# Row-by-row loads and stores on two DMA queues, in place of one queue in a written-out order, in a cross-entropy gradient kernel

## The chip, the cores and the metric

The kernel runs on one core of a Trainium2 chip. The metric is device time in microseconds (us), the median of the runs of one kernel. Beside the times there is one profiled execution, with a trace of every instruction and every DMA packet. Engines are named as in the profile: PE (matmul), DVE (vector), ACT (scalar), POOL (GpSimd), SP (the sync engine, which here does nothing but issue DMAs). A letter q behind an engine (SPq, ACTq) is its sequencer, the part that issues DMAs and waits on semaphores.

## The reference

The input is `logits`, 8 x 1024 rows of 8192 float32, and one integer label for each row. The output has the shape of `logits`: the softmax of each row, less one at the label's column.

```python
logits_max = np.max(logits, axis=-1, keepdims=True)
exp_logits = np.exp(logits - logits_max)
softmax = exp_logits / np.sum(exp_logits, axis=-1, keepdims=True)
one_hot[batch_idx, seq_idx, labels] = 1.0
return (softmax - one_hot).astype(np.float32)
```

268.4 MB are read and 268.4 MB are written, and nothing of the large input is needed twice.

## The kernel before, in words

The 8192 rows are cut into T = 64 tiles of 128 rows, one row on each of the 128 partitions. A tile is 128 x 8192 float32, that is 4 MB, 32 KB on each partition. Two tiles, 2b and 2b + 1, hold alternate rows of the same 256 (`"(b p j) v -> b p j v"` with j = 2), so that the two rows that one partition gets from such a pair lie side by side in memory, 64 KB in one piece.

All of the work is done in place in one buffer `X` with SLOTS = 6 slots of one tile each; tile t uses slot t % 6. For each tile there are five steps, in the function `compute`:

- `row_max`: DVE takes the negated maximum of each row into `m` (TENSOR_REDUCE).
- ACT computes exp(x + m) in place, and the row's sum `s` with it (ACTIVATE X<-X,m).
- DVE takes the reciprocal `r` of the sum.
- ACT multiplies the whole row by `r` in place (ACTIVATE X<-X,r). This is called the scaling below.
- DVE compares the column numbers with the row's label and subtracts the outcome from the row, in place (SCALAR_TENSOR_TENSOR X<-iota,lab,X). This is called the subtraction below.

The column numbers are 16-bit integers that stay in PSUM (`iota`); they are made once at the start in the last slot of X, which is therefore free for loads only when DVE has copied them out. On DVE the order is: reciprocal of tile t, maximum of tile t + 1, subtraction of tile t. The scaling of tile t on ACT so lies beside the maximum of tile t + 1 on DVE, and the exponential of tile t + 1 beside the subtraction of tile t. The last tile is scaled and subtracted in two halves.

No scheduler arranges anything here: the whole kernel is one critical section with semaphores set by hand. A helper, `run`, issues every instruction, with its waits ahead of it and a semaphore increment behind it. This is why nearly every instruction has the same line in the profile, L75, and why groups are told apart by their engine and tiles.

All large transfers are issued by SP on one queue, in the order that the string ORDER writes out: L is a load, S a store, the number is the tile, and W means two adjacent tiles in one transfer of 8 MB (64 KB runs in HBM):

```python
ORDER = """
L0 L1 L2W L4W S0 S1 L6 L7 S2 S3 L8 L9 S4W S6 L10W S7 S8
L12W S9 S10 L14W S11 S12 ... L52W S49 S50
L54 L55 S51 L56 S52W L57 L58 S54W L59 L60W S56 S57 L62 L63 S58W S60W S62 S63
"""
```

In the middle of the program this is one 8 MB load and two 4 MB stores in turn. SP waits at each entry for what it needs: a load for the stores that free its slots, a store for the subtraction of its tile. An entry that waits holds all entries behind it. There are 39 loads (14 of one tile, 25 of two) and 59 stores (54 and 5). The small load of the labels is issued by ACT at the start, on ACT's queue.

Of the kernel before, what the change touches and what calls it, by code (L numbers as in the profile page):

```python
# [6 lines left out]

P = 128  # L8
SLOTS = 6  # L9

ORDER = """
L0 L1 L2W L4W S0 S1 L6 L7 S2 S3 L8 L9 S4W S6 L10W S7 S8
L12W S9 S10 L14W S11 S12 L16W S13 S14 L18W S15 S16 L20W S17 S18 L22W S19 S20
L24W S21 S22 L26W S23 S24 L28W S25 S26 L30W S27 S28 L32W S29 S30 L34W S31 S32
L36W S33 S34 L38W S35 S36 L40W S37 S38 L42W S39 S40 L44W S41 S42 L46W S43 S44
L48W S45 S46 L50W S47 S48 L52W S49 S50
L54 L55 S51 L56 S52W L57 L58 S54W L59 L60W S56 S57 L62 L63 S58W S60W S62 S63
"""  # L20


@with_exitstack
def kernel(
    ctx: ExitStack,
    tc: tile.TileContext,
    logits: bass.AP,
    labels: bass.AP,
    out: bass.AP,
):  # L30
    nc = tc.nc
    fp32 = mybir.dt.float32
    i32 = mybir.dt.int32
    i16 = mybir.dt.int16
    Act = mybir.ActivationFunctionType
    Alu = mybir.AluOpType

    x_nv = logits.flatten_outer_dims()
    o_nv = out.flatten_outer_dims()
    N, V = x_nv.shape  # L40
    T = N // P
    G = 2
    B = T // G
    lab_bp = labels.rearrange("a b -> (a b)").rearrange("(b q) -> b q", q=G * P)
    x_b = x_nv.rearrange("(b p j) v -> b p j v", p=P, j=G)
    o_b = o_nv.rearrange("(b p j) v -> b p j v", p=P, j=G)

    const = ctx.enter_context(tc.tile_pool(name="const", bufs=1))
    psum = ctx.enter_context(tc.tile_pool(name="psum", bufs=1, space=bass.MemoryType.PSUM))


    X = const.tile([P, SLOTS, V], fp32)
    lab_raw = const.tile([B, G * P], labels.dtype)
    lab_f = const.tile([B, G, P], fp32)  # L54
    ident = const.tile([B, B], fp32)  # L55
    lab = const.tile([P, G, B], fp32)  # L56

    m, s, r = (const.tile([P, T], fp32, name=n) for n in ("m", "s", "r"))  # L58

    iota = psum.tile([P, V], i16)  # L60
    lab_ps = iota[:].bitcast(fp32)[:, :T].rearrange("p (j b) -> p j b", j=G)

    with tc.tile_critical():  # L63
        sem = tc.alloc_semaphore
        got = [sem(f"got{i}") for i in range(SLOTS)]
        put = [sem(f"put{i}") for i in range(SLOTS)]
        lab_got, dve, act, pe, pool = (sem(n) for n in ("lab_got", "dve", "act", "pe", "pool"))
        count = dict.fromkeys((x.name for x in (*got, *put, lab_got, dve, act, pe, pool)), 0)

        def run(engine, waits, counter, method, **operands):  # L70

            waits = list(dict.fromkeys(waits))
            for w in waits[:-1]:
                engine.wait_ge(*w)  # L74
            instruction = getattr(engine, method)(**operands)  # L75
            for w in waits[-1:]:
                instruction._wait_ge(*w)
            step = 16 if method == "dma_start" else 1
            instruction.then_inc(counter, step)
            count[counter.name] += step  # L80
            return counter, count[counter.name]


        w_raw = run(nc.scalar, [], lab_got, "dma_start", out=lab_raw[:], in_=lab_bp)
        w = run(nc.gpsimd, [], pool, "memset", ap=ident[:], constant=0.0)
        w_ident = run(
            nc.gpsimd, [w], pool, "affine_select",
            out=ident[:], in_=ident[:], compare_op=Alu.not_equal, fill=1.0,
            base=0, pattern=[[-1, B]], channel_multiplier=1,
        )  # L90

        made = X[:, SLOTS - 1, :].bitcast(i16)[:, :V]
        w_made = run(
            nc.gpsimd, [], pool, "iota", out=made, pattern=[[1, V]], base=0, channel_multiplier=0
        )
        step = mybir.dt.size(labels.dtype) // 4
        lab32 = lab_raw[:].bitcast(i32).rearrange("b (p j s) -> b j p s", j=G, s=step)
        w_lab = run(nc.vector, [w_raw], dve, "tensor_copy", out=lab_f[:], in_=lab32[:, :, :, 0])
        for j in range(G):
            w = run(  # L100
                nc.tensor, [w_ident, w_lab], pe, "transpose",
                out=lab_ps[:, j, :], in_=lab_f[:, j, :], identity=ident[:],
            )
        w = run(nc.vector, [w], dve, "tensor_copy", out=lab[:], in_=lab_ps)
        w_iota = run(
            nc.vector, [w, w_made], dve, "tensor_scalar",
            out=iota[:].bitcast(i32), in0=made.bitcast(i32), scalar1=0, scalar2=None, op0=Alu.bitwise_or,
        )


        loaded, stored, w_max, finished = {}, {-1: w_iota}, [], []

        def hbm(rows, t, n):
            b, j = divmod(t, G)
            return rows[b, :, j : j + n, :]

        def sbuf(t, n):
            return X[:, t % SLOTS : t % SLOTS + n, :]

        def load(t, n):  # L120
            free = [stored[u - SLOTS] for u in range(t, t + n) if u - SLOTS in stored]
            w = run(nc.sync, free, got[t % SLOTS], "dma_start", out=sbuf(t, n), in_=hbm(x_b, t, n))
            loaded.update(dict.fromkeys(range(t, t + n), w))

        def store(t, n):
            compute(t + n)
            w = run(
                nc.sync, [finished[t + n - 1]], put[t % SLOTS], "dma_start",
                out=hbm(o_b, t, n), in_=sbuf(t, n),
            )  # L130
            stored.update(dict.fromkeys(range(t, t + n), w))

        def row_max(t):
            w_max.append(run(
                nc.vector, [loaded[t]], dve, "tensor_reduce",
                out=m[:, t : t + 1], in_=X[:, t % SLOTS, :], axis=mybir.AxisListType.X, op=Alu.max, negate=True,
            ))

        def compute(end):

            for t in range(len(finished), end):
                x = X[:, t % SLOTS, :]
                if t == 0:
                    row_max(0)
                w = run(
                    nc.scalar, [w_max[t]], act, "activation",
                    out=x, in_=x, func=Act.Exp, bias=m[:, t : t + 1], scale=1.0, accum_out=s[:, t : t + 1],
                )
                w = run(nc.vector, [w], dve, "reciprocal", out=r[:, t : t + 1], in_=s[:, t : t + 1])
                if t + 1 < T:  # L150
                    row_max(t + 1)

                n = 1 if t + 1 < T else 2
                cols = [slice(i * V // n, (i + 1) * V // n) for i in range(n)]
                scaled = [
                    run(
                        nc.scalar, [w], act, "activation",
                        out=x[:, c], in_=x[:, c], func=Act.Copy, bias=0.0, scale=r[:, t : t + 1],
                    )
                    for c in cols  # L160
                ]
                for c, w in zip(cols, scaled):
                    w = run(
                        nc.vector, [w], dve, "scalar_tensor_tensor",
                        out=x[:, c], in0=iota[:, c], scalar=lab[:, t % G, t // G : t // G + 1], in1=x[:, c],
                        op0=Alu.is_equal, op1=Alu.subtract, reverse1=True,
                    )
                finished.append(w)

        for word in ORDER.split():  # L170
            n = 2 if word.endswith("W") else 1
            (load if word[0] == "L" else store)(int(word[1:].rstrip("W")), n)
        for w in dict.fromkeys(stored[t] for t in range(T - SLOTS, T)):
            nc.sync.wait_ge(*w)


# [28 lines left out]
```

## Time and profile before

| What | Value |
|---|---|
| Median of 3 runs | 1253.62 us (1253.48 to 1255.25) |
| The profiled execution's own time | 1253.48 us |
| Its span in the profile | 1251.7 us, 582 instructions |
| DVE busy | 1119.1 us, 196 instructions |
| ACT busy | 919.0 us, 194 instructions |
| POOL and PE busy | 7.4 us and 0.4 us |
| Moved between HBM and SBUF | 268.50 MB read, 268.44 MB written, 429 GB/s over the span |
| Granted clock | 1.0 |

The span is the time in which the profile shows instructions; the execution's own time is 1.78 us longer. Shares of busy time are averages over the span. The chain of work that ended last, which the profile follows back from the last instruction, tells which of the resources set the end. A DMA's packets are its pieces as the DMA engines carry them: here one packet for each partition of a transfer, of 32 KB or 64 KB, and a packet of 4 bytes for each of the 16 DMA engines that increments the semaphore.

### The profile page before, as it was taken

What the parts mean: (1) busy time and instruction counts of PE and PEld (TensorE: products, weight loads), DVE (VectorE), ACT (ScalarE), POOL (GpSimd) and SP (SyncE); (2) the same over time, 40 slices, a digit from 0 to 9 for tenths busy, and PEclk for the clock granted to TensorE, in tenths of its full rate; (3) what the DMA queues carried; (4) which work ended last, traced back from release to release, by engine and by line L of the source; (5) the groups of instructions that cost most, each with busy time, mean ns of one, the idle gap of its engine ahead of it and who ended that gap; (6) DMA issues with size and microseconds to landing.
All of it is one profiled execution on the core that took longest, in us unless ns stands there. A gap on an engine that the chain in (4) does not pass through costs nothing.

```text
span 1251.7 us, 582 instructions
## 1 busy us (share of the span) xinstructions
PE 0.4 (0%) x2; PEld 0.3 (0%) x2; DVE 1119.1 (89%) x196; ACT 919.0 (73%) x194; POOL 7.4 (1%) x7
## 2 busy tenths in 40 slices
PE   0000000000000000000000000000000000000000
PEld 0000000000000000000000000000000000000000
DVE  5999999888998889988899888898888989997993
ACT  3888887667777777777777777877768778887782
POOL 2000000000000000000000000000000000000000
DMA  9999999999999999999999999999999999999998
GB/s 404 419 436 431 438 422 435 434 427 431 430 448 434 418 429 436 441 421 430 430 435 439 434 431 426 432 450 429 425 429 436 437 427 432 419 424 436 435 436 354
DMA packets 14165, 536.98 MB, mean 429 GB/s; under 512 B 1584, under 2 KB 1584, under 8 KB 1616
## 3 DMA queue, kind: packets, MB, share of 16 engines
q1 hardware_dynamic: 14112, 536.88, 99.6%
q10 hardware_dynamic: 48, 0.07, 0.0%
q14 instruction: 5, 0.04, 0.0%
HBM read 268.50 MB, written 268.44 MB: 429 GB/s over the span
## 4 chain that ended last, share of the span: by engine, by line
DMA 58%; DVE 39%; ACT 1%; issue 0%; PE 0%; ACTq 0%; DVEq 0%; SPq 0%
DMA out_dram<-X 30%; DMA X<-in_logits_dram 28%; DVE X L75 19%; DVE m L75 19%; ACT X L75 1%; DVE iota L75 0%; DMA lab_raw<-in_labels_dram 0%; DVE lab_f L75 0%; DVE r L75 0%; PE iota L75 0%; DVE lab L75 0%; ACTq L200 0%; DVEq L74 0%; SPq L63 0%
## 5 line engine op out<-in xcount | busy, mean ns | idle before, releaser
L75 DVE TENSOR_REDUCE m<-X 128x1 f32<-128x8192 f32 x64 | 555.2, 8674 | 100.0 <-DMA X<-in_logits_dram 100.0
L75 ACT ACTIVATE X<-X,m 128x8192 f32<-128x8192 f32 x64 | 455.8, 7122 | 214.3 <-DVE m L75 214.3
L75 DVE SCALAR_TENSOR_TENSOR X<-iota,lab,X 128x8192 f32<-128x8192 int16 (+1 forms) x65 | 559.6, 8610 | 3.8 <-ACT X L75 3.8
L75 ACT ACTIVATE X<-X,r 128x8192 f32<-128x8192 f32 (+1 forms) x65 | 456.0, 7016 | 95.6 <-DVE r L75 95.6
L75 DVE RECIPROCAL r<-s 128x1 f32<-128x1 f32 x64 | 9.8, 153 | 7.3 <-ACT X L75 7.3
L75 ACT ACTIVATION_READ_ACCUMULATOR X<-X,m 128x1 f32 x64 | 11.9, 187 | 0.0
L75 DVE CAST lab_f<-lab_raw 32x256 f32<-32x256 int32 x1 | 3.7, 3661 | 4.7 <-DMA lab_raw<-in_labels_dram 4.7
L75 POOL IOTA X<- 128x8192 int16 x1 | 6.9, 6943 | 0.0
L75 DVE TENSOR_SCALAR iota<-X 128x4096 int32<-128x4096 int32 x1 | 4.4, 4428 | 0.1
L75 ACT ACT_TABLE_LOAD x1 | 1.3, 1283 | 1.3 <-SPq L63 1.3
L75 DVE COPY lab<-iota 128x64 f32<-128x64 f32 x1 | 0.2, 225 | 0.5 <-PE iota L75 0.5
L75 PE MATMUL iota<-ident,lab_f 32*128 32x32 f32 x2 | 0.4, 300 | 8.4 <-DVE lab_f L75 8.4
L75 PEld LDWEIGHTS iota<-ident,lab_f 32*128 32x128 f32 x2 | 0.3, 195 | 8.4 <-DVE lab_f L75 8.4
L75 POOL TENSOR_SCALAR_AFFINE_SELECT ident<-ident 32x32 f32<-32x32 f32 x1 | 0.2, 203 | 0.1
L75 POOL MEMSET ident<- 32x32 f32 x1 | 0.1, 114 | 0.5 <-SPq L63 0.5
L189 POOL MEMSET const-bfloat16-1.0<- 128x1 bf16 x1 | 0.1, 106 | 0.0
L189 POOL MEMSET const-uint8-127<- 128x1 uint8 x1 | 0.1, 106 | 0.0
L189 POOL MEMSET const-float32-0.0<- 128x1 f32 x1 | 0.1, 103 | 0.2 <-issue 0.2
L189 POOL MEMSET const-float32-1.0<- 128x1 f32 x1 | 0.1, 103 | 0.0
## 6 DMA issues: line engine op xcount, KB each, us to landing
out_dram<-X SPq DMA_DIRECT2D x54, 4096.0 KB, 24.9
X<-in_logits_dram SPq DMA_DIRECT2D x14, 4096.0 KB, 19.6
X<-in_logits_dram SPq DMA_DIRECT2D x25, 29.0
out_dram<-X SPq DMA_DIRECT2D x5, 26.6
lab_raw<-in_labels_dram ACTq DMA_DIRECT2D x1, 64.0 KB, 3.8
```

The lines of the kernel that those rows point to most:

```text
L75: instruction = getattr(engine, method)(**operands)
L189: nc = _bacc.Bacc("TRN2", target_bir_lowering=False, num_devices=1)
```

## The change

ORDER and everything that reads it go away. SP issues the 64 loads alone, one tile each, in the order of the tiles; a load waits for nothing but the store that frees its slot. The 64 stores, one tile each, are issued by ACT on its own queue. In ACT's stream the store of tile t - 1 stands between the exponential of tile t and the scaling of tile t, and waits there for the subtraction of tile t - 1. The final wait for the last six stores moves from SP to ACT. The order and the kind of the instructions on DVE, PE and POOL are the same as before, as are those on ACT apart from the stores. The layout of rows and the six slots stay, too. The helper's line is L64 in the new kernel.

```diff
-ORDER = """
-L0 L1 L2W L4W S0 S1 L6 L7 S2 S3 L8 L9 S4W S6 L10W S7 S8
...
-"""
         def store(t, n):
-            compute(t + n)
             w = run(
-                nc.sync, [finished[t + n - 1]], put[t % SLOTS], "dma_start",
+                nc.scalar, [finished[t + n - 1]], put[t % SLOTS], "dma_start",
                 out=hbm(o_b, t, n), in_=sbuf(t, n),
             )
...
-        def compute(end):
...
+        load(0, 1)
+        row_max(0)
+        for t in range(T):
+            x = X[:, t % SLOTS, :]
+            w = run(
+                nc.scalar, [w_max[t]], act, "activation",
+                out=x, in_=x, func=Act.Exp, bias=m[:, t : t + 1], scale=1.0, accum_out=s[:, t : t + 1],
+            )
+            w = run(nc.vector, [w], dve, "reciprocal", out=r[:, t : t + 1], in_=s[:, t : t + 1])
+            if t + 1 < T:
+                load(t + 1, 1)
+                row_max(t + 1)
+            if t > 0:
+                store(t - 1, 1)
...
-        for word in ORDER.split():
-            n = 2 if word.endswith("W") else 1
-            (load if word[0] == "L" else store)(int(word[1:].rstrip("W")), n)
+            finished.append(w)
+        store(T - 1, 1)
         for w in dict.fromkeys(stored[t] for t in range(T - SLOTS, T)):
-            nc.sync.wait_ge(*w)
+            nc.scalar.wait_ge(*w)
```

More of the change, by code (lines that the diff above doesn't have):

```diff
@@ L9 @@
 SLOTS = 6
-ORDER = """
-L0 L1 L2W L4W S0 S1 L6 L7 S2 S3 L8 L9 S4W S6 L10W S7 S8
[L15 to L19, printed above, removed]
-"""
 @with_exitstack
@@ L137, in row_max @@
             ))
-        def compute(end):
[L141 to L144, printed above, removed]
+        load(0, 1)
[12 more added lines that the diff above has]
+                store(t - 1, 1)
+            n = 1 if t + 1 < T else 2
+            cols = [slice(i * V // n, (i + 1) * V // n) for i in range(n)]
+            scaled = [
+                run(
+                    nc.scalar, [w], act, "activation",
+                    out=x[:, c], in_=x[:, c], func=Act.Copy, bias=0.0, scale=r[:, t : t + 1],
+                )
+                for c in cols
+            ]
+            for c, w in zip(cols, scaled):
@@ L145, in compute @@
                 w = run(
-                    nc.scalar, [w_max[t]], act, "activation",
-                    out=x, in_=x, func=Act.Exp, bias=m[:, t : t + 1], scale=1.0, accum_out=s[:, t : t + 1],
-                )
[L149 to L167, printed above, removed]
@@ L168, in compute @@
-                finished.append(w)
-        for word in ORDER.split():
-            n = 2 if word.endswith("W") else 1
-            (load if word[0] == "L" else store)(int(word[1:].rstrip("W")), n)
+                    nc.vector, [w], dve, "scalar_tensor_tensor",
+                    out=x[:, c], in0=iota[:, c], scalar=lab[:, t % G, t // G : t // G + 1], in1=x[:, c],
+                    op0=Alu.is_equal, op1=Alu.subtract, reverse1=True,
+                )
+            finished.append(w)
+        store(T - 1, 1)
```

## The prediction

> **What bounds the kernel now.** I read the page's busy line, its DMA lines and queues first, then the chain of waits, then windows by stage, and the timeline where the stores begin.
>
> ```profile
> PE 0.4 (0%) x2; PEld 0.3 (0%) x2; DVE 1119.1 (89%) x196; ACT 919.0 (73%) x194; POOL 7.4 (1%) x7
> DMA packets 14165, 536.98 MB, mean 429 GB/s; under 512 B 1584, under 2 KB 1584, under 8 KB 1616
> q1 hardware_dynamic: 14112, 536.88, 99.6%
> ```
>
> The 16 DMA engines carry SP's queue (q1) for 99.6% of the span; DVE comes next with 89%. The chain agrees, and the waits show who is behind:
>
> ```profile
> DMA 58%; DVE 39%; ACT 1%; issue 0%; PE 0%; ACTq 0%; DVEq 0%; SPq 0%
> ...
> DVE m L75 <- DMA X<-in_logits_dram: 100.0, 25, 4.9
> SPq L75 <- DVE r L75: 733.5, 55, 33.0
> SPq L75 <- DMA out_dram<-X: 444.1, 32, 33.1
> ```
>
> DVE waits for loads 25 times, 100.0 us in all: it is 100 us quicker than the transfers. SP's long waits cost nothing while the queue still holds a transfer. By stage, in the windows (the last two columns are the DMA share and GB/s):
>
> ```profile
> 168.00:638.00 470.00, 0.00 (x0) 0.00 (x0) 417.18 (x75) 344.32 (x73) 0.00 (x0) 1.00 1.00 432
> 638.00:986.00 348.00, 0.00 (x0) 0.00 (x0) 312.17 (x55) 257.79 (x54) 0.00 (x0) 1.00 1.00 434
> 986.00:1100.00 114.00, 0.00 (x0) 0.00 (x0) 108.97 (x21) 91.96 (x19) 0.00 (x0) 1.00 1.00 426
> 1200.00:1252.00 52.00, 0.00 (x0) 0.00 (x0) 31.77 (x7) 25.74 (x7) 0.00 (x0) 1.00 0.88 379
> ```
>
> Only start and end lie below 426 GB/s. So the time is bytes, by the rate of the engines, plus small losses. The trace's packet records give these. The median 32 KB packet takes 1.213 us, the 64 KB one 2.418, the 4-byte one 0.009; a load's packet and a store's are equal. For one of 16 engines: 8704/16 x 1.213 + 3840/16 x 2.418 + 98 x 0.009 = 659.9 + 580.3 + 0.9 = 1241.1 us. The records sum to 1247.1, so 6.0 us are excess over the medians: 0.3 in the first packets, 5.7 later. The first large packet starts at 2.2, the last ends at 1249.9: 1247.7 us, of which 0.6 idle. After it 1.8 us are left to the span's end, and the execution's time lies another 1.8 above the span. The median of the runs is 0.14 above this execution.
>
> **The change, part by part.** *Smaller transfers.* All 128 are of one tile, where 98 were: 1024 packets of 1.213 and 128 of 0.009 on each engine, 1242.1 + 1.2 = 1243.3 us, 2.2 more than 1241.1. Nothing covers this, since these engines are the bound.
>
> *The stores on ACT.* An issue takes 0.33 us on SP (row below) and 0.41 on ACT (the labels' load). In the timeline at the first store:
>
> ```profile
> 38.20 8.74 DVE L75 SCALAR_TENSOR_TENSOR X<-iota,lab,X 128x8192 f32<-128x8192 int16 x1
> 38.31 7.12 ACT L75 ACTIVATE X<-X,m 128x8192 f32<-128x8192 f32 x1 [1.46 <-DVE m L75]
> ...
> 46.85 0.15 DVE L75 RECIPROCAL r<-s 128x1 f32<-128x1 f32 x1
> 46.92 8.67 DVE L75 TENSOR_REDUCE m<-X 128x1 f32<-128x8192 f32 x1
> ...
> 47.04 7.12 ACT L75 ACTIVATE X<-X,r 128x8192 f32<-128x8192 f32 x1 [1.51 <-DVE r L75]
> ...
> 1129.76 0.34 SPq L75 DMA_DIRECT2D out_dram<-X  x1
> ```
>
> The new wait on ACT is for the subtraction of tile t - 1; behind it are queued the scaling of t and the exponential of t + 1. But the scaling waits for the reciprocal of t, which DVE runs just after that very subtraction (46.85 behind 38.20 + 8.74), so the wait ends no later than one that ACT had. Only the issue is new: the scaling starts 0.4 us late, at 47.4, and ends at 54.5, while DVE is in its maximum until 55.6. The 1.46 us that ACT waits for that maximum are the cover. Without it, it would be 63 x 0.41 = 26 us of ACT, still within DVE's 100 us of waiting. I take 0. On SP, 64 loads stay; none is behind a store any more.
>
> *The freed order.* A load waits for its slot alone. In the steady stage let a load land at A. Maximum 8.7, then the subtraction of the tile before 8.7 (it stands behind that maximum), then the wait for the next load at A + 19.4 (two 4 MB transfers of 8 x 1.213 = 9.7 each), then 17.4 again: the store is issued at A + 36.8. A slot comes round every 6 x 19.4 = 116.4 us, so 79.6 remain for its store and next load; sharing the engines by halves each takes 19.4, 38.8 together. Some 40 us are spare, less a few for issue and landing: a second transfer waits in each queue most of the time, and the engines never run dry. What is late next is the DMA again.
>
> *The end.* When stores begin, at 47, 4.6 loads are done; 1.4 remain, and at half rate the last lands 27 us later. That lead of 27 us from a load's issue to its landing then keeps itself, since a load is issued as often as a store lands. So tile 63 lands 27 us after store 57, with 4.6 stores still to do: 45 us. DVE needs only 8.7 + 7.2 for maximum and exponential, the older subtraction until 17.4, then halves of 3.7, 4.4 and 4.4: the last store is issued at 30, and three stores lie ahead of it until 35. No idle: 0.
>
> *Load and store packets in turn.* Today the queue changes direction 59 times (counted in ORDER). Afterwards both queues are busy for all but 4.6 loads at the start and 4.6 stores at the end: 118.8 transfers, 950 packets on each engine. The trace never has two large streams at once, so I bound the price by its changes. All excess behind the first packets put on the 59 changes is 5.7/59 = 0.096 us for each and engine; in the even stretch from 638 to 986 us it is 0.49 us for 18 changes, 0.027. The changes afterwards number 950, if the engines alternate by packet, or 119, if by whole transfer. The four products are 3.2, 11.4, 25.6 and 91 us. Below nothing: a load writes SBUF while a store reads it, so two streams could overlap; the end of that is DVE's own time. Its last subtraction ends at 1235.5; less 100.0 of waits 1135.5, plus 14.7 to the landing of a store (shortest of the DMA view) and 1.5: a span of 1152, 96 us below 1247.6, the sum below before this term. The equal packets of both directions speak for a cap inside the engine and so against such a gain. Between the four products, with no row nearer to one than to another, I take their geometric middle, 17 us.
>
> The Trainium skill, page "DMA: Bandwidth & Descriptors", section "Queues, rings and completion order", says that an engine goes round its queues packet by packet, a packet there being typically 9 to 17 descriptors. A transfer here has 8 pieces and one semaphore write on each engine, so by that rule it would be the coarse count, 3 to 11 us, and a time of about 1253 to 1261; no view of before shows two large queues at once.
>
> *Sum.* 2.2 (start) + 0.3 (first packets) + 1243.3 + 17 + 1.8 = 1264.6 us of span; + 1.8 + 0.14 gives 1266.5.
>
> **The rivals.** *Alternation is free.* The 5.7 us of excess and 0.6 of idle belong to the old queue's restarts and vanish: 2.2 + 0.3 + 1243.3 + 1.8 = 1247.6, a time of 1249.5, 4.1 below before. For it: between 638 and 986 us nine cycles of one 8 MB load and two stores take 348.36/9 = 38.71 us against 38.78 of packet work, though each has two changes. Against: in the stretch before, twelve take 39.13. It decides below 4.1 us for 950 packets, 4.3 ns each: then the change is a gain. Chance 0.20 (0.14 a gain over 0.2%, 0.06 within).
>
> *The directions overlap.* Down to 1152 + 1.9 = 1154 if DVE is the bound. Chance 0.06.
>
> *Stores get more than half.* Then a load's lead grows, and little is left to store when tile 63 lands. With only stores 62 and 63 left, the engines idle from store 62's end (17.4 + 9.7) to 30 and before 17.4: 20 us, 1249.5 + 20 = 1269.5. For it: nothing seen; against: equal packets. It decides below 3.1 stores left. Chance 0.06.
>
> *Every change at the dearer price, by packet:* 1249.5 + 91 = 1341. Against: the even stretch has 0.027. Chance 0.08.
>
> The change does what it says: the order of instructions shows 64 loads on SP and 64 stores on ACT.
>
> **How the numbers follow.** The forecast, alternation at a price of 3 to 60 us, has 0.60 and by itself reaches from 1253 to 1310; 0.04 of it lies within 0.2% (2.5 us, about what a measurement of this kernel can tell from no change). Faster: 0.14 + 0.06 = 0.20. Same: 0.06 + 0.04 = 0.10. Slower: 0.56 + 0.06 + 0.08 = 0.70. The range goes from 1247, under the free rival, to 1305; outside lie 0.06 below, and above it the 0.08 and some 0.04 of the forecast.
>
> **What would show it.** The forecast: two queues of about 268 MB each, a mean near 424 GB/s, DVE's wait for loads up from 100 to about 115 us, and 32 KB packets whose excess is spread evenly from 50 to 1220 us. Wrong about ACT: the scaling shows up late in DVE's waits (DVE X on ACT far over 3.8 us). Wrong about the end: an idle DMA in the last two slices beyond today's 354 GB/s. Wrong altogether: a rate of 430 GB/s or more in the middle, or DVE without waits for loads.

## The result, and the profile after

The changed kernel is faster, by half a per cent: 1248.1 us median (1247.97 to 1248.16, 4 runs) against 1254.2 for the kernel before beside it, a ratio of 0.9951 with a 95% interval of 0.9933 to 0.9968. A later set of runs gave 1248.12 against 1254.31, ratio 0.9950 (0.9937 to 0.9962). The forecast was 1266.5 and slower. The rival "alternation is free" had said 1249.5, with a chance of 0.14 for a gain of this size. The time lies inside the range of 1247 to 1305, on the other side of the kernel before.

The page's busy line, the slices, and the packets by queue (number, MB, share of the 16 engines' span):

```profile
span 1246.4 us, 592 instructions
PE 0.4 (0%) x2; PEld 0.3 (0%) x2; DVE 1121.3 (90%) x196; ACT 919.0 (74%) x194; POOL 7.4 (1%) x7
...
GB/s 406 418 430 433 435 434 430 433 435 433 431 434 434 433 431 434 434 432 431 434 435 432 431 434 434 431 433 434 435 431 433 433 434 432 432 433 435 431 432 385
DMA packets 18484, 536.98 MB, mean 431 GB/s; under 512 B 2064, under 2 KB 2064, under 8 KB 2096
q1 hardware_dynamic: 9216, 268.44, 50.0%
q10 hardware_dynamic: 9264, 268.51, 49.9%
```

The bytes are the same, and each queue carries half. The DMA engines are as full as before, 99.9% in sum, but no slice from the third to the last but one is below 430 GB/s. The same stages as before, in the windows:

```profile
168.00:638.00 470.00, 0.00 (x0) 0.00 (x0) 435.90 (x78) 361.18 (x76) 0.00 (x0) 1.00 1.00 433
638.00:986.00 348.00, 0.00 (x0) 0.00 (x0) 312.64 (x55) 257.20 (x55) 0.00 (x0) 1.00 1.00 433
986.00:1100.00 114.00, 0.00 (x0) 0.00 (x0) 103.60 (x17) 84.09 (x18) 0.00 (x0) 1.00 1.00 433
```

Where 432, 434 and 426 stood, 433 stands three times. The last slice of the page has 385 GB/s; it was 354. The waits of ACT and DVE:

```profile
ACT X L64 <- DVE m L64: 187.9, 64, 19.7
ACT X L64 <- DVE r L64: 116.0, 64, 2.1
DVE m L64 <- DMA X<-in_logits_dram: 91.4, 47, 2.6
...
DVE X L64 <- ACT X L64: 4.1, 1, 4.1
```

DVE's wait for loads is down from 100.0 to 91.4 us, in 47 short pieces in place of 25 longer ones. DVE still waits for the transfers, so the bound is where it was.

**Where the 5.3 us went.** Both profiled executions have the same 1.8 us outside the span, so the spans differ as the times of these two do, by 5.3 (the medians differ by 6.1). From the first large packet to the end of the last it was 1247.68 us (2.18 to 1249.86) and is 1242.40 (2.38 to 1244.78). I add up the packet records for the average of the 16 engines, in us. "Excess" is what packets took over the medians of 1.213 and 2.418; "gaps" is time with no large packet, with the semaphore packets in it; neighbouring records overlap by some 3 ns, which is taken off. A record does not name its engine; each packet is taken to follow the one at whose end it starts, and gaps less overlap do not depend on this.

| | packets at the median | excess | gaps | overlap | sum |
|---|---|---|---|---|---|
| before | 1240.19 | 5.96 | 4.03 | -2.50 | 1247.68 |
| after | 1242.11 | 1.35 | 2.14 | -3.20 | 1242.40 |
| difference | +1.92 | -4.61 | -1.89 | -0.70 | -5.28 |

Of the gaps, 2.86 us lay behind 1200 us before and 1.38 lie there now. Ahead of 1200 us there were only 1.2 us of them, and 0.8 now: that the one queue was starved by SP's waits explains little. So 4.6 us are packets that no longer take too long, 1.5 are engines that idle less at the end, and the smaller packets cost 1.2 (1.92 less 0.70).

Of the 1.35 us of excess that is left, 0.97 lies at 48.8 to 51.2 us, where the first store starts beside the loads. Before had 1.01 at 58.4, where its first store came. Behind 65 us the changed kernel has 0.16 us of excess, the kernel before 4.65.

A second number shows what excess does. A transfer's semaphore is raised by each of the 16 engines as its share lands; the time from the first of the 16 to the last is the spread of the landing. Before, it grew from 0.3 us at 23 us to 6.3 at 1047 and was 3.7 for the last store. After, it is 0.5 at 23 us, 2.3 at the most and 2.1 for the last store. An engine that loses time stays behind, and a transfer is done when its slowest engine is.

### The profile page after: what moved, and what is told of

It reads as the page before. It is cut to its first block, busy times and chain, and to the rows that moved or that the text cites. A ratio compares the mean times of both kernels' runs of the same rounds, so it can differ in the third digit from the quotient of the medians.

```text
span 1246.4 us, 592 instructions
## 1 busy us (share of the span) xinstructions
PE 0.4 (0%) x2; PEld 0.3 (0%) x2; DVE 1121.3 (90%) x196; ACT 919.0 (74%) x194; POOL 7.4 (1%) x7
## 4 chain that ended last, share of the span: by engine, by line
another core or an unknown queue 69%; DVE 21%; DMA 6%; SPq 1%; ACT 1%; DVEq 0%; issue 0%; PE 0%; ACTq 0%
DVE m L64 10%; DVE X L64 10%; DMA out_dram<-X 4%; DMA X<-in_logits_dram 2%; SPq L64 1%; ACT X L64 1%; DVE iota L64 0%; DVEq L52 0%; DMA lab_raw<-in_labels_dram 0%; DVE lab_f L64 0%; DVE r L64 0%; PE iota L64 0%; ACTq L64 0%; DVE lab L64 0%
## 5 line engine op out<-in xcount | busy, mean ns | idle before, releaser
L64 DVE TENSOR_REDUCE m<-X 128x1 f32<-128x8192 f32 x64 | 555.6, 8681 | 91.4 <-DMA X<-in_logits_dram 91.4
L64 ACT ACTIVATE X<-X,m 128x8192 f32<-128x8192 f32 x64 | 455.8, 7122 | 187.9 <-DVE m L64 187.9
L64 DVE SCALAR_TENSOR_TENSOR X<-iota,lab,X 128x8192 f32<-128x8192 int16 (+1 forms) x65 | 559.6, 8610 | 4.1 <-ACT X L64 4.1
L64 ACT ACTIVATE X<-X,r 128x8192 f32<-128x8192 f32 (+1 forms) x65 | 456.0, 7016 | 116.0 <-DVE r L64 116.0
L64 DVE RECIPROCAL r<-s 128x1 f32<-128x1 f32 x64 | 9.8, 153 | 7.3 <-ACT X L64 7.3
L64 ACT ACTIVATION_READ_ACCUMULATOR X<-X,m 128x1 f32 x64 | 11.9, 186 | 0.0
L64 DVE CAST lab_f<-lab_raw 32x256 f32<-32x256 int32 x1 | 3.5, 3526 | 4.9 <-DMA lab_raw<-in_labels_dram 4.9
L64 POOL IOTA X<- 128x8192 int16 x1 | 6.9, 6943 | 0.0
L64 DVE TENSOR_SCALAR iota<-X 128x4096 int32<-128x4096 int32 x1 | 4.4, 4427 | 0.1
L64 DVE COPY lab<-iota 128x64 f32<-128x64 f32 x1 | 0.2, 224 | 0.5 <-PE iota L64 0.5
L64 PE MATMUL iota<-ident,lab_f 32*128 32x32 f32 x2 | 0.4, 300 | 8.5 <-DVE lab_f L64 8.5
L64 PEld LDWEIGHTS iota<-ident,lab_f 32*128 32x128 f32 x2 | 0.3, 196 | 8.4 <-DVE lab_f L64 8.4
L64 POOL TENSOR_SCALAR_AFFINE_SELECT ident<-ident 32x32 f32<-32x32 f32 x1 | 0.2, 202 | 0.1
L64 POOL MEMSET ident<- 32x32 f32 x1 | 0.1, 114 | 0.5 <-SPq L52 0.5
## 6 DMA issues: line engine op xcount, KB each, us to landing
X<-in_logits_dram SPq DMA_DIRECT2D x64, 4096.0 KB, 24.2
out_dram<-X ACTq DMA_DIRECT2D x64, 4096.0 KB, 55.1
```

## The experiments

The change has two halves that can be had apart: single tiles in place of pairs, and two queues in place of one. The written order is a third. Theory A put the loss of the kernel before on the changes of direction inside one queue, theory B on the 64 KB packets, theory C on the late, irregular part of the written order.

**e1: the same order on one queue, single tiles.**

```diff
-L0 L1 L2W L4W S0 S1 L6 L7 ...
+L0 L1 L2 L3 L4 L5 S0 S1 L6 L7 ...
```

> The kernel before with each transfer of two tiles split into two of one tile, in the same order on the same one queue: 128 transfers, still 59 changes of direction. Theory A (a change of direction within one queue costs about 0.1 us on each engine, and two queues hide it): the excess of the packets stays near 6 us and the time at 1253 to 1255. Theory B (the 64 KB packets are what is slow): excess near 1.3 us as in the changed kernel, time 1248 to 1250. Theory C (the written-out order runs the queue dry in its last part, 986 us on): as A, 1253 to 1255, with the loss in the same late places.

Measured: 1254.92 us, ratio 1.0004 (0.9995 to 1.0013). Excess 5.06 us, of which 3.67 behind 65 us; the landings spread by up to 8.5 us. B falls: on one queue pairs or single tiles make no difference. In the windows the late part is again the weak one:

```profile
986.00:1100.00 114.00, 0.00 (x0) 0.00 (x0) 98.51 (x19) 86.02 (x18) 0.00 (x0) 1.00 1.00 433
1100.00:1200.00 100.00, 0.00 (x0) 0.00 (x0) 96.00 (x17) 74.75 (x16) 0.00 (x0) 1.00 1.00 426
```

**e2: one queue, a load and a store in turn.**

```diff
-ORDER = """L0 L1 L2W L4W S0 S1 L6 L7 S2 S3 ...
+ORDER = """L0 L1 L2 L3 L4 L5 S0 S1 L6 S2 L7 S3 L8 S4 ... L63 S59 S60 S61 S62 S63
```

> One queue, single tiles, order L0 to L5, S0 S1, then L6 S2 L7 S3 and so on: 117 changes of direction in place of 59 (59 of them from load to store, in place of 30), and no hand-made late part. Theory A (each change costs in one queue): the excess from load to store doubles, 3 us more than before, less about 3 us of the old order's late part and end: 1253 to 1257, and above the changed kernel's 1248.1 in any case by 4 us or more. Theory B (64 KB packets): 1248 to 1250. Theory C (the old order's late part): 1248 to 1250, with excess only at the first store.

Measured: 1251.72 us, ratio 0.9978 (0.9970 to 0.9987). It lies between all the expectations: 2.6 us below before, 3.6 above the two queues. The slices:

```profile
GB/s 404 420 431 432 428 430 433 426 428 430 434 432 432 432 432 435 432 434 435 432 432 434 432 434 435 434 430 434 433 434 435 433 431 434 433 434 433 433 431 360
```

Behind the first two slices the low ones, 426 to 428, are all in the first 290 us; from there on it streams like the two queues until the last slice, 360. The packet records agree: of 3.96 us of excess 2.56 lie behind 65 us, and only 0.43 of these behind 310 us. They sit in clusters some 19.4 us apart, on packets at the end of a load where a store follows. But most of the 59 such changes came after 310 us and cost next to nothing, 0.43 us together. So A falls as it stood: a change from load to store does not cost by itself, even inside one queue. What ended with the excess was the drift of the engines: the landings' spread grew from 0.4 us to 5.2 by 358 us and then stayed there to the end. At the end the engines stop that much apart, with 3.1 us of gaps. C is right for a part: with the regular order 2.6 us are gone.

**e3: two queues, loads two tiles at a time.**

```diff
-                load(t + 1, 1)
+                if t == 0:
+                    load(1, 1)
+                elif (t + 1) % 2 == 0:
+                    load(t + 1, 2)
```

> The changed kernel with the loads from tile 2 on issued two tiles at a time (64 KB packets), stores as they are, two queues. Theory A (two queues hide the changes): 1247 to 1249, excess near 1.3 us. Theory B (64 KB packets are slow): excess back, 3 us or more, time 1251 to 1254. Theory C: 1247 to 1249. Where the engines take turns by packet, loads of 64 KB get two thirds of the rate while both queues are full.

Measured: 1266.09 us, ratio 1.0095 (1.0082 to 1.0109), which none of the theories had. The slices show where:

```profile
GB/s 400 430 399 415 431 441 439 431 443 418 443 432 436 440 417 429 446 436 434 438 415 446 432 425 437 429 431 438 427 430 434 433 437 429 439 428 430 438 350 265
```

In the middle the rate is what it was; with 64 KB packets single slices swing, as they did in the kernel before. The last two slices have 350 and 265: 15.6 us of gaps on each engine there. In the timeline of the end:

```profile
1203.95 8.69 DVE L64 TENSOR_REDUCE m<-X 128x1 f32<-128x8192 f32 x1 [4.16 <-DMA X<-in_logits_dram]
...
1251.67 0.34 ACTq L64 DMA_DIRECT2D out_dram<-X  x1
```

Tiles 62 and 63 land together, at 1203.9. DVE then has two tiles to do, and the last store is issued 47.7 us later, while the 18.4 MB that were left to store need only some 43 us and also come in pieces. With single loads it is one tile and 30.4 us (below).

**e4: the changed kernel again**, beside these three.

> The changed kernel as it is, on the chip and beside the runs of the others: 1248.1, ratio 0.995. All theories agree; it is the yardstick for the three others.

Measured: 1248.12 us (1247.98 to 1248.26), ratio 0.9950 (0.9937 to 0.9962). The kernel before went from 1252.79 to 1256.88 beside it, so the single queue is not only slower but also less even.

**e5: as e3, the last eight tiles loaded one by one.**

```diff
+                elif t + 1 >= T - 8:
+                    load(t + 1, 1)
                 elif (t + 1) % 2 == 0:
                     load(t + 1, 2)
```

> The two-queue kernel with loads of two tiles, but the last eight tiles loaded one by one. If the 16 us of idle DMA at the end of the run with wide loads (two tiles land at once at 1204, and only stores 60 to 63 are left) are what made it slow: the end idle falls below 5 us and the time to 1249 to 1255. If the unequal sharing of the engines costs all the way: 1262 to 1267.

Measured: 1250.93 us, ratio 0.9979 (0.9969 to 0.9990). The last slice has 385 GB/s, as in the changed kernel, and the gaps behind 1200 us are 1.28 us. So 15 of e3's 18 us over the changed kernel were its end. Of the other 3, 2.3 are excess in the first 100 us, 3.4 us in e3 and 3.5 in e5 against 1.2 in the changed kernel, at the start of the wide loads and of the stores. Behind 100 us wide loads still leave 1.7 and 1.0 us of excess, against 0.16.

**e6: the changed kernel with four slots.**

```diff
-SLOTS = 6
+SLOTS = 4
```

> The changed kernel with four slots in place of six. By the working of the prediction a slot's round is 36.8 us from landing to store plus 38.8 us for store and load at half rate, 75.6, plus a few us for issue and landing; four slots give 4 x 19.4 = 77.6. So nothing is spare: 19.4 to 20.2 us for each tile, 1250 to 1302, the queues at times dry, and far less waiting in ACT's queue (stores land in 20 to 25 us in place of 55). Were slots not what feeds the queues: 1248, and landing times as before.

Measured: 1311.21 us, ratio 1.0458 (1.0431 to 1.0485), 9 us over the top of what was expected. The issues (median us from issue to landing) of this kernel, then of the changed one:

```profile
X<-in_logits_dram SPq DMA_DIRECT2D x64, 4096.0 KB, 21.5
out_dram<-X ACTq DMA_DIRECT2D x64, 4096.0 KB, 21.7
```

```profile
X<-in_logits_dram SPq DMA_DIRECT2D x64, 4096.0 KB, 24.2
out_dram<-X ACTq DMA_DIRECT2D x64, 4096.0 KB, 55.1
```

A store takes 21.7 us with four slots and 55.1 with six: the difference is waiting in ACT's queue, and that waiting is the stock that keeps the engines fed. Without it the queues run dry again and again: a pause of over 5 us between load packets comes 26 times, between store packets 32 times, and in the changed kernel never. And there the excess is back, 32 us of it in two queues, beside 32 us of gaps. (e7 below, whose queues run dry too, has 44 us.) So two queues are free of excess only while both are full.

**e7: the store ahead of the exponential on ACT.**

```diff
+            if t > 0:
+                store(t - 1, 1)
             w = run(nc.scalar, [w_max[t]], act, "activation", out=x, in_=x, func=Act.Exp, ...)
...
-            if t > 0:
-                store(t - 1, 1)
```

> The changed kernel with the store of tile t - 1 issued by ACT ahead of the exponential of tile t, in place of behind it. The store waits for the subtraction of t - 1, which DVE runs behind the maximum of t, so the exponential can no longer lie beside the subtraction: for each tile 8.6 + 8.7 on DVE, then 0.4 for the issue and 7.3 for the exponential, then 0.2: 25.2 us, 64 of them and 30 at the start, 1600 to 1650 us, with DVE idle about 8 us a tile waiting for ACT. If the wait on ACT cost nothing wherever it stands: 1248.

Measured: 1635.86 us, ratio 1.3047 (1.3019 to 1.3075), as expected. The waits:

```profile
ACT X L64 <- DVE X L64: 661.7, 63, 10.5
DVE r L64 <- ACT X L64: 490.1, 64, 7.7
```

ACT stands 10.5 us a tile for the subtraction, and then DVE 7.7 us for the exponential. In the changed kernel neither row exists for more than one tile.

**e8 and e9: one queue in turn, engines out of step from the start; e10: the yardstick.** Theory D was formed on e2: excess comes when the engines go over from load to store in step. Small loads of 1 to 15 partitions come first, which use as many engines (1 to 15 add up to 120, and e8 has 120 semaphore packets more than e2). In e9:

```diff
+        p = 0
+        for k in range(15, 0, -1):
+            w_stagger = run(
+                nc.sync, [], stagger, "dma_start", out=X[p : p + k, 4, :5120], in_=x_nv[0:k, 0:5120]
+            )
+            p += k
```

In e8 the loop ran upward, with 2048 columns, into a buffer of its own.

> The one queue with loads and stores in turn, with 15 small loads ahead (1 to 15 partitions of 8 KB, into a tile that nothing uses), which give the 16 DMA engines from 0 to 15 packets of about 0.3 us: the engines are out of step by 4 to 5 us from the start. In the run without it the packets' excess behind the first store was 2.7 us, all of it before 350 us, until the engines' landings had drifted 5 us apart. Theory D (the excess comes from engines that change from load to store in step): under 1 us of excess behind the first store. Theory E (it comes from the time, the addresses or the first rounds): 2 to 3 us as before. The time itself is no test, since the added loads cost 2.3 us on the average engine and 4.5 on the busiest: 1250 to 1257.

> As the staggered run, but the 15 small loads go in falling order (15 partitions down to 1) with 20 KB rows of about 0.76 us each, into slot 4 before tile 4 needs it: the engines should start tile 0 up to 6 us apart, in even steps, where the first try gave 2.2 us. Theory D (excess comes from engines that change from load to store in step): behind the first store under 0.7 us of excess. Theory E (first rounds, time or addresses): 2 to 3 us, as in the plain run, until about 350 us. The added loads cost 5.7 us on the average engine and 11 on the busiest, so the time, 1255 to 1265, is no test.

> The plain one-queue run with loads and stores in turn once more, as the yardstick for the staggered one: 1251 to 1253 us. If its excess is a property of the order, it is again about 2.7 us behind the first store, over by 350 us, and the landings drift apart to about 5 us; if it comes by chance, it is another amount at another time.

Measured: e8 1260.09, e9 1284.21, e10 1251.76 us. The time of e9 says nothing: its small loads were far slower than thought, 22 us over what was reckoned, all before 38 us. What matters is the excess afterwards, when the first stores are through in all of them:

| | spread of landings at 50 to 110 us | at 1100 us | excess behind 65 us | behind 123 us |
|---|---|---|---|---|
| e2, plain | 0.4 to 0.8 | 5.2 | 2.56 | 2.15 |
| e10, plain again | 0.3 to 0.7 | 5.2 | 1.96 | 1.51 |
| e8 | 2.0 to 2.6 | 5.7 | 1.32 | 1.02 |
| e9 | 10.5 to 10.6 | 5.6 | 1.93 | 0.25 |
| changed kernel | 0.8 to 0.9 | 2.2 | 0.16 | 0.16 |

e10 says that the excess belongs to the order and is not chance. e8 came out between the two expectations, with a stagger of less than half the size meant. In e9 the first store is issued at 81 us, but the second only at 98.5, and by then the queue has run dry on eight engines. They stand idle, 1.4 us on the average of all 16, and go on together at 99.4. Then come 1.7 us of excess up to 123 us, while the spread falls from 10.5 to 5.4; from there on it is 0.25. The loss at the first store, 0.5 and 0.9 us in e2 and e10, is under 0.1 in e8 and e9.

So with this order there is less excess where the engines are further apart, which speaks for D. e1 speaks against it: between 638 and 986 us its landings were 4.5 to 7.5 us apart, and its excess there was 0.85 us, where e2, at 5.2 us apart, had 0.05 and the kernel before, at 5.0 to 5.9, had 0.49. The small loads also disturbed the start. D is not settled.

## Why the prediction was wrong, step by step

**Smaller transfers: +2.2 us, measured 1.2 in the large packets.** Neighbouring records run into each other by 3 ns, so two 32 KB packets take 2.420 us, and one of 64 KB takes 2.414: with 240 of these on each engine before, that is the 1.2 us. e1 confirms that this term is small.

**Stores on ACT: 0, right.** The wait of ACT for the reciprocal grew from 95.6 to 116.0 us, 63 times 0.32, and its wait for the maximum shrank by 26.4. DVE's wait for ACT stayed at 4.1 us. The first store in the timeline, in the place that the prediction had worked out:

```profile
46.97 0.36 ACTq L64 DMA_DIRECT2D out_dram<-X  x1
47.38 7.12 ACT L64 ACTIVATE X<-X,r 128x8192 f32<-128x8192 f32 x1 [1.85 <-DVE r L64]
55.51 8.74 DVE L64 SCALAR_TENSOR_TENSOR X<-iota,lab,X 128x8192 f32<-128x8192 int16 x1
55.63 7.12 ACT L64 ACTIVATE X<-X,m 128x8192 f32<-128x8192 f32 x1 [1.12 <-DVE m L64]
```

The scaling starts at 47.4, and of the 1.46 us of cover 1.12 are left. e7 shows that this is the place of the store's wait, not a property of waits on ACT.

**The freed order: right.** The 79.6 us for a store and a load are 55.1 + 24.2 = 79.3 in the DMA view, and e6 shows what the spare time was worth.

**The end: right.** Tile 63 landed at 1199.2, where 4.6 stores were left by their bytes (45.6 us to the last packet), and the last store went out 30.4 us later:

```profile
1199.19 8.69 DVE L64 TENSOR_REDUCE m<-X 128x1 f32<-128x8192 f32 x1 [1.94 <-DMA X<-in_logits_dram]
...
1229.60 0.34 ACTq L64 DMA_DIRECT2D out_dram<-X  x1
```

The end now even gains 1.5 us of gaps, because the engines arrive less far apart. The prediction had not looked at that.

**Load and store packets in turn: 17 us, measured none. This is the step that failed.** It took the 5.7 us of excess of the old queue, laid all of it on its 59 changes of direction, and multiplied the price by the 119 or 950 changes to come. The engines do take turns at the finest grain: in the records each engine carries one 32 KB packet of q1 and one of q10, in turn, each of 1.213 us. Each semaphore write takes a turn of its own, so that some 830 of these turns are a change from a data packet of one queue to one of the other, seven times the coarse count. And behind 65 us there are 0.16 us of excess in all: the changes cost nothing. The prediction's own sign of being wrong altogether, 430 GB/s or more in the middle, came with 433. The evidence against the price was in the prediction, as the point for its rival: nine cycles of 38.71 us with two changes each, against 38.78 of packet work. A price of 0.027 us worked out of a stretch whose cycles show no loss at all is noise, and the geometric middle of four products, none of which was a price that a change had shown, gave it weight.

The Trainium skill, page "DMA: Bandwidth & Descriptors", section "Queues, rings and completion order", which the prediction had cited, says that an engine drains a packet of typically 9 to 17 descriptors from one queue before it turns to the next. Here it turned after each 32 KB piece, eight times in a transfer. The measurement decides; the count was the fine one, and the price at this grain was nothing.

**What the excess was instead.** The runs show three parts. One is the written order, 2.6 us of time that one queue in regular turn also saves (e2); of its excess 1.33 us stand in one place, between 1050 and 1100 us, in the late, irregular part, and in e1 1.23 us between 1150 and 1200, in the late part too. In both places the queue also ran dry on some of the engines, with 0.3 and 0.4 us of gaps. One is a start that every run but e8 and e9 has, 0.5 to 1.1 us of excess at the first store, which nearly cancels in the comparison. The rest of the difference, 3.6 us from e2 to the changed kernel, is excess that one queue shows while its engines move apart, 2.6 and 2.0 us in e2 and e10 behind 65 us, and the drift that goes with it, with 3.1 and 3.3 us of gaps at the end in place of 1.4. That two full queues with equal packets do not have this excess is shown. Why an engine loses time where a load ends and a store begins in the same queue, and not where the two are in different queues, is not; the changed kernel's engines are in step within 2.3 us all the time, so step alone is not the cause.

The rival "alternation is free" had the sign and the size. Of its 1.4 us too much, 1.2 are in the stretch from the first packet to the last, 1242.4 where 0.3 + 1243.3 had been put. That it came so near is luck in part. The 0.6 us of idle time that it let vanish were 4.0 us of gaps less 0.9 of semaphore packets and 2.5 of overlap; gaps and excess shrank but did not vanish, to 2.1 and 1.4 us, and 3.2 us of overlap, which no sum had, nearly made up for them. That the time lies inside the stated range is no merit of the forecast: its lower end came from this rival. The rival that the directions overlap is out: 433 GB/s in the middle is no more than the even stretch before, 434.

## What to carry to other kernels

A loss that sits at an event is not the event's price: look first for a stretch that has the event without the loss, and trust that stretch before multiplying. With loads and stores in equal pieces on two queues, this kernel, bound by its transfers, needed no written order, but it needed enough slots for both queues to hold a second transfer, and single-tile loads at the end. A store may be issued by a computing engine at no cost where that engine would wait anyway for what comes just behind the data, and at a third of the run time where it would not.

## What the runs showed of the hardware that was not expected

- The 16 DMA engines need not stay in step. On one queue the landings of one transfer drifted up to 6.3 us apart (8.5 in e1), on two full queues with equal packets 2.3; with 64 KB loads (e5) it was up to 6.4, with four slots (e6) 4.1. In the one-queue runs in regular turn the spread stopped growing at 5.2 us, twice, and the excess with it.
- The first store of a run stretches the load packets beside it by about 1 us on each engine, in the kernel before (1.01) and in the changed one (0.97). It does not in e8 and e9, whose engines were 2.2 and 10.5 us apart by then (under 0.1).
- Two full queues whose packets are equal are served one for one, with a turn for each semaphore write. Packets of 32 KB, 1.210 us apart, cost only 0.2% more than packets of 64 KB, 2.414 apart.
